# Products over 512 columns of weights in the gate stages and output projections of a two-layer decoder trunk

## The chip, the cores and the metric

The kernel runs on one core of one Trainium2 chip, in one launch. The metric is device time in microseconds (us). The five engines are TensorE (PE for matmuls, PEld for its weight loads), VectorE (DVE), ScalarE (ACT), GpSimd (POOL) and SyncE (SP, which issues the DMAs). They run beside each other and wait for each other by semaphores.

## The reference

x is 1024 tokens by 1024 channels, float32. The parts that the change touches are these, per layer:

```python
h = rmsnorm(x, norm_mix_pre[l])
if l % 2 == 0:                                     # layer 0
    proj = h @ w_in_even[e]
    qa, fa, ia, ga, ub, vb = jnp.split(proj, splits, axis=-1)   # 512 columns each
    oa = hgrn2_mix(qa, fa, ia, ga, ...)            # gated recurrence, ends with norm(o) * silu(ga)
    ob = chunk_gmlp_mix(gelu(ub), gelu(vb), ...)   # u * (W_s layernorm(v) + b), chunks of 128 tokens
    mix = jnp.concatenate([oa, ob], axis=-1) @ w_out_even[e]
else:                                              # layer 1
    mix = dilated_attention_mix(h, w_in_odd[o], positions) @ w_out_odd[o]
x = x + rmsnorm(mix, norm_mix_post[l])
h = rmsnorm(x, norm_ffn_pre[l])
y = jnp.square(jax.nn.relu(h @ w_ff1[l])) @ w_ff2[l]            # hidden size 4096
x = x + rmsnorm(y, norm_ffn_post[l])
```

## The kernel before

Every product is made of three matmuls in a short float32 format (fp32r): a weight or activation is split into a high part and the rest, and `mm3` (L624) adds hi·hi, hi·lo and lo·hi in one PSUM bank of 512 words. A weight piece is loaded by SP into a raw tile, ACT copies the high part, DVE or POOL subtracts it to get the rest (`load_piece`, L565). HT holds the layer's normalised input, transposed (channels as rows), in both parts.

`gemm_nat` (L631) is the product with tokens as rows: a 128x128 piece of HT is stationary, columns of weights move, and 8 channel blocks x 3 parts make 24 matmuls for one block of 128 tokens (t = 0 to 7). `gemm_tr` (L641) is the other way about: weights are stationary and 512 tokens move.

Layer 0's mixer (L844) has these stages in order: the value projection (256 columns a time), the recurrence in four heads (hgrn) with b products between its steps, then the stages b (gate input v, columns B0, normalised and mixed over the chunk: `gmlp_mix`), u (`gemm_tr`) and g (columns G0: the output gate of the recurrence, after which the two halves of the mixer's result are transposed into HT: `to_HT`, `ob_to_HT`). b and g are `gemm_nat` stages over 512 columns, which are taken as two runs of 256 (list `blocks`, L877): first all eight t for the first half, then all eight for the second. The output projection (L1374 to L1403) makes for each t and each half hf of the 1024 columns two `gemm_nat` products over 256 columns into the two halves of one bank; `post_part` squares and copies each bank, and after both halves the block's sum of squares, residual, second norm and h follow (`prenorm`), h is stored to DRAM (hd) and transposed into HT (`h_to_HT`). In layer 1 oT, the transposed attention output, is reloaded into HT from DRAM while the output projection has begun. Then `ff1` starts: hidden units are made in blocks i of 1024 (of 4096) from weights loaded as R tiles of 128x8x256 words (2048 words), each by two DMAs of 512 KB (`ff1_weights`, L1425); ACT copies and DVE subtracts a unit tile's two parts (128x1024 each) before its products start.

SBUF is handed out in numbered blocks: 17 of 1024 words, two of 2048 (b17 and b18) and some others (b7_14296 is tile 14296 in block 7). A tile gets a block when all earlier users of the block are done. R tiles need 2048 words, so only b17 and b18 take them.

All operations go through a recorder (`Plan`): the program first writes down every operation, and a list scheduler then gives them out at build time engine by engine, by readiness under a cost model, so that the order on each engine is fixed when the kernel runs. All instructions are issued at L422 (`emit`), which is the line that the profile shows. The names in it are the tiles: WP the ring of split weights, b the numbered blocks, mm, tr, pa, pb the banks.

Of the kernel before, what the change touches and what calls it, by code (L numbers as in the profile page):

```python
# [8 lines left out]
F32 = mybir.dt.float32  # L9
F32R = mybir.dt.float32r  # L10
# [474 lines left out]
class Trunk:  # L485
# [145 lines left out]
    def gemm_nat(self, t, w, c0, width, o=None):  # L631

        if o is None:
            o = self.mm_bank()[:, :width]
        ts = slice(t * P, (t + 1) * P)
        for k in range(NK):
            self.mm3(o, self.HT[:, 0, k, ts], self.HT[:, 1, k, ts],
                     w[0][k][0][:, c0:c0 + width], w[0][k][1][:, c0:c0 + width], k == 0, k == NK - 1)
        return o
# [204 lines left out]
    def layer0_mix(self):  # L844
# [3 lines left out]
        with nc.pool() as pl:  # L848
# [24 lines left out]
            for t, b in order:  # L873
                o = self.gemm_nat(t, wv[b], 0, 256)
                nc.scalar.activation(oa[t][:, b * 256:(b + 1) * 256], o, AF.Copy, scale=0.5)
            self.wfree(*wv)
            blocks = [("b", B0), ("b", B0 + 256), ("u", U0), ("u", U0 + 256), ("g", G0), ("g", G0 + 256)]  # L877
            ph = nc.pool()
            for h in range(4):
                state = None  # L880
                nxt = None
                for b in range(2):
                    fps = self.gemm_tr(b, wf, P)
                    qps = self.gemm_tr(b, wf, 0)
                    if b == 1:
                        self.wfree(wf)
                        nxt = (self.load_cols(w, [Q0 + (h + 1) * P, F0 + (h + 1) * P], P) if h < 3
                               else self.load_cols(w, [blocks[0][1]], 256))
# [6 lines left out]
            pl2.reserve("gz256", 256, F32, 2)  # L895
            vs = [pl2.tile([P, 512], F32, name="vs", bufs=NT) for t in range(NT)]
            ob = [[pl.tile([P, 2, 512], F32, name=f"ob{i}{j}") for j in range(2)] for i in range(2)]
            sums = {}
            for n, (kind, c0) in enumerate(blocks):
                nxt = None  # L900
                if n + 1 < len(blocks):
                    nxt = self.load_cols(w, [blocks[n + 1][1]], 256)
                else:
                    self.wout = [self.load_cols(a["w_out_even"][0], [256 * i], 256) for i in range(2)]
                half = n % 2
                cs = slice(half * 256, half * 256 + 256)
                if n == 2:
                    pl2.__exit__()
                    pl2 = nc.pool(2)
                if kind == "u":  # L910
                    for hf in range(2):
                        for j in range(2):
# [3 lines left out]
                            o = ob[hf][half][:, j]  # L916
                            nc.gpsimd.tensor_tensor(o, o, u, op=OP.mult)
                else:
                    for t in range(NT):
                        x = self.gemm_nat(t, cur, 0, 256)  # L920
                        if kind == "b":
                            if half == 0:
                                sums[t] = self.small(2)
                            self.gelu2(pl2, vs[t][:, cs], x, accum=sums[t][:, half:half + 1])
                            if half == 1:
                                self.gmlp_mix(t, ob, self.gmlp_norm(pl2, vs[t], sums[t]))
                        else:
                            if half == 0:
                                self.onorm(pl2, oa[t])
                            th = pl2.tile([P, 256], F32, name="th", tag="th", bufs=2)  # L930
# [892 lines left out]
```

## Time and profile before

| | |
|---|---|
| time, median of 3 runs | 2390.89 us (2390.3 to 2392.29) |
| time of the profiled execution | 2387.89 us |
| its span | 2385.8 us (2.09 us lie around it) |
| mean granted clock of PE | 0.988 of 2.4 GHz |
| busy: PE, PEld | 2291.6 us (96%), 2003.9 us (84%) |
| busy: DVE, ACT, POOL | 1627.4 us (68%), 1120.8 us (47%), 1095.5 us (46%) |

The busy share of PE is the mean over stages. The stages lie in the span as follows: layer 0's recurrence to 232 us, its stages b, u and g to 371, its output projection to 477, its feed-forward to 1098; layer 1's attention to 1595, output projection to 1728, feed-forward to the end. In a row of the timeline the first number is the start, the second the time until the last of the group ends, and the bracket at the end is the time that the engine idled before, with who released it.

### The profile page before, as it was taken

The numbers are of one execution on the slowest core, as the hardware profiler recorded it, in microseconds if no ns is written. First come the engines' busy times: TensorE is split into PE (matmuls) and PEld (weight loads), VectorE is DVE, ScalarE is ACT, GpSimd is POOL, SyncE is SP. The second block draws the span as 40 slices with busy tenths as digits, with TensorE's granted clock in tenths as the row PEclk, the third lists the DMA queues.
The fourth block names the chain that finished last, engine by engine and source line by source line (L and its number), as shares of the span: only waits on it lengthen the run. The fifth ranks groups of instructions, "written<-read, shape, count | busy, mean of one in ns | idle before, by whom it ended". The sixth has DMA issues, their size and how long they took to land.

```text
span 2385.8 us, 35511 instructions
## 1 busy us (share of the span) xinstructions
PE 2291.6 (96%) x12490; PEld 2003.9 (84%) x12490; DVE 1627.4 (68%) x3130; ACT 1120.8 (47%) x2429; POOL 1095.5 (46%) x1192
## 2 busy tenths in 40 slices
PE   8999999998999999999999999998998999999998
PEld 7888889976888878887999999988976888888887
DVE  6687875545555686748888788876645555778747
ACT  6444435442232343335777777787432223434333
POOL 2111343255655889415555455443245655555204
PEclk9999999999999999999999999999999999999999
DMA  5110123344444776854311111115444444678654
GB/s 186 54 36 19 36 71 121 142 167 156 158 146 150 242 249 240 287 192 155 102 48 51 46 47 52 46 57 176 167 147 158 160 150 150 251 274 285 220 175 166
DMA packets 229178, 342.33 MB, mean 143 GB/s; under 512 B 15220, under 2 KB 110472, under 8 KB 229000
## 3 DMA queue, kind: packets, MB, share of 16 engines
q1 hardware_dynamic: 229000, 340.07, 42.3%
q8 instruction: 98, 1.61, 0.3%
q14 instruction: 80, 0.66, 0.1%
HBM read 240.92 MB, written 99.09 MB: 143 GB/s over the span
## 4 chain that ended last, share of the span: by engine, by line
PE 74%; DVE 11%; POOL 4%; ACT 4%; DMA 4%; issue 2%; SPq 0%; DVEq 0%; POOLq 0%; ACTq 0%
PE mm L422 37%; PE pa L422 18%; PE pb L422 11%; DVE b L422 9%; PE tr L422 9%; POOL b L422 4%; ACT b L422 3%; DMA b<-hd 1%; DVE WP L422 1%; DMA b<-oTd 1%; DVE HT L422 1%; DMA b<-in_w_in_odd_dram 1%; ACT WP L422 1%; ACT HT L422 0%; DMA b<-in_w_ff_dram 0%
## 5 line engine op out<-in xcount | busy, mean ns | idle before, releaser
L422 POOL TENSOR_TENSOR b<-b,b 128x512 f32<-128x512 f32 (+5 forms) x522 | 590.3, 1146 | 750.4 <-ACT b L422 367.2
L422 PE MATMUL mm<-WP,HT 128*128 128x256 f32 (+2 forms) x4704 | 830.8, 323 | 7.4 <-DVE HT L422 3.2
L422 PEld LDWEIGHTS mm<-WP,HT 128*128 128x128 f32 x4704 | 710.4, 190 | 51.3 <-DVE HT L422 4.4
L422 ACT ACTIVATE b<-b 128x512 f32<-128x512 f32 (+6 forms) x659 | 326.0, 509 | 392.2 <-DVE b L422 158.8
L422 POOL TENSOR_TENSOR b<-b 128x512 f32<-128x512 f32 (+4 forms) x354 | 314.6, 894 | 334.7 <-DVE b L422 222.0
L422 ACT ACTIVATE WP<-b 128x1024 fp32r<-128x1024 f32 (+2 forms) x248 | 194.7, 792 | 350.8 <-PE pb L422 167.1
L422 DVE TENSOR_TENSOR WP<-b,WP 128x1024 fp32r<-128x1024 f32 (+1 forms) x164 | 234.6, 1436 | 150.6 <-ACT WP L422 150.3
L422 DVE TENSOR_TENSOR b<-b,b 128x1024 fp32r<-128x1024 f32 (+6 forms) x360 | 246.9, 703 | 123.1 <-ACT b L422 75.8
L422 ACT ACTIVATE b<-mm 128x512 f32<-128x512 f32 (+3 forms) x374 | 161.9, 445 | 263.4 <-PE mm L422 227.3
L422 PE MATMUL mm<-HT,b 128*128 128x512 f32 x1056 | 262.2, 399 | 17.3 <-ACT b L422 17.3
L422 PEld LDWEIGHTS mm<-HT,b 128*128 128x128 f32 x1056 | 200.4, 192 | 59.9 <-ACT b L422 19.3
L422 DVE TENSOR_TENSOR HT<-b,HT 128x1024 fp32r<-128x1024 f32 (+3 forms) x131 | 206.3, 1586 | 21.8 <-ACT HT L422 21.8
L422 PE MATMUL tr<-b,b 128*128 128x128 f32 x1074 | 176.6, 285 | 40.9 <-DVE b L422 33.8
L422 PE MATMUL pa<-WP,HT 128*128 128x512 f32 x768 | 193.7, 390 | 0.0
L422 DVE TENSOR_TENSOR b<-tr,b 64x128 fp32r<-64x128 f32 (+5 forms) x404 | 162.6, 407 | 36.2 <-ACT b L422 29.2
L422 PEld LDWEIGHTS tr<-b,b 128*128 128x128 f32 x1074 | 132.0, 150 | 61.5 <-DVE b L422 38.5
L422 PE MATMUL tr<-WP,HT 128*128 128x512 f32 x672 | 172.3, 394 | 6.7 <-ACT WP L422 3.6
L422 PEld LDWEIGHTS pa<-WP,HT 128*128 128x128 f32 x768 | 144.4, 188 | 30.0
L422 ACT ACTIVATE HT<-b 128x1024 fp32r<-128x1024 f32 (+4 forms) x147 | 142.1, 973 | 55.7 <-PE mm L422 23.5
L422 PE MATMUL pa<-WP,b 128*128 128x512 f32 x672 | 162.0, 389 | 0.0
L422 PEld LDWEIGHTS tr<-WP,HT 128*128 128x128 f32 x672 | 127.2, 190 | 34.6 <-ACT WP L422 4.0
L422 PE MATMUL pa<-b,b 128*128 128x128 f32 (+3 forms) x624 | 146.4, 333 | 5.5 <-DVE b L422 4.8
(62 smaller groups left out, 2872.8 us busy)
## 6 DMA issues: line engine op xcount, KB each, us to landing
b<-in_w_ff_dram SPq DMA_DIRECT2D x176, 512.0 KB, 4.8
hc<-b SPq DMA_DIRECT2D x224, 256.0 KB, 2.1
b<-hc SPq DMA_DIRECT2D x112, 512.0 KB, 5.5
b<-hd SPq DMA_DIRECT2D x56, 256.0 KB, 3.2
b<-in_w_in_odd_dram SPq DMA_DIRECT2D x64, 192.0 KB, 2.8
x<-b SPq DMA_DIRECT2D x24, 512.0 KB, 2.6
b<-x SPq DMA_DIRECT2D x24, 512.0 KB, 4.1
b<-in_w_in_even_dram SPq DMA_DIRECT2D x32, 256.0 KB, 2.8
```

Of the source, the lines that this page charges most:

```text
L422: return getattr(self.real[eng], meth)(*[x.real() if isinstance(x, View) else x for x in a], **{k: x.real() if isinstance(x, View) else x ...
```

## The change

Stages b and g are one run of 512 columns each instead of two of 256 (the list `blocks` carries a width), and each output projection product goes over 512 columns: 2304 matmuls of 128x256 become 1152 of 128x512 (384 each in the two gate stages together, in layer 0's output projection, and in layer 1's). What follows a product in b and g is done once on 512 columns instead of twice on 256 (gelu and its sum; tanh, add, multiply), and the add of the two half sums goes. w_out is loaded in four quarters (512 columns by half of the channels) in place of four runs of 256 columns. The quarter "wide", which lies outside the WP ring, is two tiles of 2048 words in place of four of 1024: b17 and b18. In layer 0 it is the quarter that the first half's products end with, (0, 1); in layer 1 it is (1, 1), which the second half's products end with.

```diff
--- before.py
+++ after.py
...
-    def gemm_nat(self, t, w, c0, width, o=None):
-
-        if o is None:
-            o = self.mm_bank()[:, :width]
+    def gemm_nat(self, t, w, width):
+
+        o = self.mm_bank()[:, :width]
         ts = slice(t * P, (t + 1) * P)
         for k in range(NK):
-            self.mm3(o, self.HT[:, 0, k, ts], self.HT[:, 1, k, ts],
-                     w[0][k][0][:, c0:c0 + width], w[0][k][1][:, c0:c0 + width], k == 0, k == NK - 1)
+            self.mm3(o, self.HT[:, 0, k, ts], self.HT[:, 1, k, ts], *w[k], k == 0, k == NK - 1)
         return o
...
-            blocks = [("b", B0), ("b", B0 + 256), ("u", U0), ("u", U0 + 256), ("g", G0), ("g", G0 + 256)]
+            blocks = [("b", B0, 512), ("u", U0, 256), ("u", U0 + 256, 256), ("g", G0, 512)]
...
-            sums = {}
-            for n, (kind, c0) in enumerate(blocks):
+            for n, (kind, c0, width) in enumerate(blocks):
                 nxt = None
                 if n + 1 < len(blocks):
-                    nxt = self.load_cols(w, [blocks[n + 1][1]], 256)
+                    nxt = self.load_cols(w, [blocks[n + 1][1]], blocks[n + 1][2])
                 else:
-                    self.wout = [self.load_cols(a["w_out_even"][0], [256 * i], 256) for i in range(2)]
-                half = n % 2
-                cs = slice(half * 256, half * 256 + 256)
-                if n == 2:
+                    self.wout = {(0, 0): self.load_cols(a["w_out_even"][0], [0], 512, (0, 2))}
...
-                        x = self.gemm_nat(t, cur, 0, 256)
+                        x = self.gemm_nat(t, cur[0], 512)
                         if kind == "b":
-                            if half == 0:
-                                sums[t] = self.small(2)
-                            self.gelu2(pl2, vs[t][:, cs], x, accum=sums[t][:, half:half + 1])
-                            if half == 1:
-                                self.gmlp_mix(t, ob, self.gmlp_norm(pl2, vs[t], sums[t]))
+                            s = self.small()
+                            self.gelu2(pl2, vs[t], x, accum=s)
+                            self.gmlp_mix(t, ob, self.gmlp_norm(pl2, vs[t], s))
                         else:
-                            if half == 0:
-                                self.onorm(pl2, oa[t])
-                            th = pl2.tile([P, 256], F32, name="th", tag="th", bufs=2)
+                            self.onorm(pl2, oa[t])
+                            th = pl2.tile([P, 512], F32, name="th", tag="th", bufs=2)
                             nc.scalar.activation(th, x, AF.Tanh, scale=0.5)
                             nc.vector.scalar_tensor_tensor(th, th, 1.0, x, op0=OP.add, op1=OP.mult)
-                            nc.gpsimd.tensor_tensor(oa[t][:, cs], oa[t][:, cs], th, op=OP.mult)
-                            if half == 1:
-                                self.to_HT(t, [oa[t][:, k * P:(k + 1) * P] for k in range(4)], t % 2 == 1)
-                                self.ob_to_HT(t, ob)
+                            nc.gpsimd.tensor_tensor(oa[t], oa[t], th, op=OP.mult)
+                            self.to_HT(t, [oa[t][:, k * P:(k + 1) * P] for k in range(4)], t % 2 == 1)
+                            self.ob_to_HT(t, ob)
...
-                    wnext = self.load_cols_lazy(self.a["w_out_odd"][0], [0], 256)
+                    wnext = self.load_cols_lazy(self.a["w_out_odd"][0], [0], 512, (0, 2))
...
-        self.wout = [wcur, self.load_cols_lazy(self.a["w_out_odd"][0], [256], 256)]
-        for x in self.wout:
+        self.wout = {(0, 0): wcur, (0, 1): self.load_cols_lazy(self.a["w_out_odd"][0], [0], 512, (4, 6))}
+        for x in self.wout.values():
...
-            self.wout.append(self.load_cols(wo, [512], 256))
-            self.wout.append(self.load_cols(wo, [768], 256, buf=[
-                pl.tile([P, 1024], F32R, name="wide", tag=f"wide{j}", bufs=1) for j in range(4)]))
+            wide = [pl.tile([P, 2048], F32R, name="wide", tag=f"wide{j}", bufs=1) for j in range(2)]
+            for x in ((0, 0), (0, 1), (1, 0), (1, 1)):
+                if x not in self.wout:
+                    buf = wide if x == ((1, 1) if l else (0, 1)) else None
+                    self.wout[x] = self.load_cols(wo, [512 * x[0]], 512, (4 * x[1], 4 * x[1] + 2), buf)
             n = 3 * l
             ss = {}
             for t, hf in sorted(((t, hf) for t in range(NT) for hf in range(2)), key=lambda x: (max(0, x[0] + 1 - n), x[1], x[0])):
-                bank = self.mm_bank()
-                for i in range(2):
-                    self.gemm_nat(t, self.wout[2 * hf + i], 0, 256, bank[:, 256 * i:256 * i + 256])
+                bank = self.gemm_nat(t, self.wout[hf, 0][0] + self.wout[hf, 1][0], 512)
...
-            self.wfree(*self.wout[:3])
+            self.wfree(*self.wout.values())
```

The scheduler gives out a new order. On SP, the loads of R tiles stand elsewhere. Before, in layer 1, two of them (here the second) were issued among the reloads of oT, a hundred microseconds ahead of ff1:

```order
L422 DMA oTd_71<-b18_6777 128x512 [waits DVE_49]
L422 DMA b19_14458<-oTd_71 128x4x128 [waits DMAHW0_49,DVE_49]
L422 DMA b7_14296<-oTd_71 128x4x128 [waits DMAHW6_49,DMAHW1_49,DVE_49]
L422 DMA b18_14731<-in_w_ff1_dram 128x4x256 [waits DMAHW7_49,DMAHW4_49]
L422 DMA b18_14731<-in_w_ff1_dram 128x4x256
L422 DMA b19_14458<-oTd_71 128x4x128 [waits DMAHW5_49,DVE_49]
L422 DMA b7_14296<-oTd_71 128x4x128 [waits DMAHW6_49,DMAHW2_49,DVE_49]
```

After, the first two stand behind the store of h of the seventh block (b12_13731 to hd_82; b17 and b18 are the blocks that wide held) and wait for PE, the last reader of wide:

```order
L422 DMA x3_70<-b0_13848 128x1024 [waits DMAHW3_49,DVE_49]
L422 DMA hd_82<-b12_13731 128x1024 [waits DMAHW0_49,DVE_49]
L422 DMA b17_14499<-in_w_ff1_dram 128x4x256 [waits PE_49,Pool_49]
L422 DMA b17_14499<-in_w_ff1_dram 128x4x256 [waits DMAHW2_49]
L422 DMA b18_14508<-in_w_ff1_dram 128x4x256 [waits PE_49,Pool_49]
L422 DMA b18_14508<-in_w_ff1_dram 128x4x256
L422 DMA x3_70<-b1_13859 128x1024 [waits DMAHW6_49,DMAHW5_49,DVE_49]
```

Both R pairs have moved behind wide's last matmul, which in layer 1 is the last one of the output projection. In layer 0 two R pairs, which SP issued at 49.24 us and among the loads of the g stage, likewise moved behind the last matmul on wide there, in the first half (hf = 0) of the eighth block.

On PE, at the end of the recurrence of layer 0 (pb, tr are its own matmuls, mm the b products), before:

```order
L422 MATMUL pb_81<-b9_542,b13_231 128x128 [waits DVE_49]
L422 MATMUL pb_81<-b2_94,b4_432 128x128
L422 MATMUL tr_78<-b2_94,b7_570 128x128 [waits Activation_49]
L422 MATMUL tr_77<-b2_94,b7_570 128x128
L422 MATMUL pb_81<-b19_689,b13_231 128x128 [waits DVE_49]
L422 MATMUL pb_81<-b2_94,b4_432 128x128
L422 MATMUL pb_81<-b19_689,b13_231 128x128 [waits DVE_49]
L422 MATMUL pb_81<-b3_95,b4_432 128x128
L422 MATMUL tr_78<-b3_95,b7_570 128x128
L422 MATMUL pb_81<-b9_542,b13_231 128x128 [waits DVE_49]
L422 MATMUL pb_81<-b3_95,b4_432 128x128
L422 MATMUL mm_76<-WP_67,HT_63 128x256 [waits DVE_49]
```

and after:

```order
L422 MATMUL tr_78<-b2_94,b7_570 128x128 [waits Activation_49]
L422 MATMUL tr_77<-b2_94,b7_570 128x128
L422 MATMUL mm_75<-WP_67,HT_63 128x512 x6
L422 MATMUL pb_81<-b19_687,b13_231 128x128 [waits DVE_49]
L422 MATMUL pb_81<-b2_94,b4_432 128x128
L422 MATMUL pb_81<-b19_687,b13_231 128x128 [waits DVE_49]
L422 MATMUL pb_81<-b3_95,b4_432 128x128
L422 MATMUL tr_78<-b3_95,b7_570 128x128
L422 MATMUL mm_75<-WP_67,HT_63 128x512 x3
L422 MATMUL mm_76<-WP_67,HT_63 128x512 x3
L422 MATMUL pb_81<-b9_542,b13_231 128x128 [waits DVE_49]
L422 MATMUL pb_81<-b3_95,b4_432 128x128
```

The three mm banks were full before, and the next b product waited for DVE to empty one; after, b products stand between the recurrence's steps to its end.

On PE, in layer 1's output projection, the transposes of the first block's h (tile b1_14522 before), before:

```order
L422 MATMUL mm_74<-WP_67,HT_63 128x256 [waits Activation_49]
L422 MATMUL mm_74<-WP_67,HT_63 128x256 x23
L422 MATMUL mm_74<-b5_14659,HT_63 128x256 x6
L422 MATMUL mm_74<-b2_14697,HT_63 128x256 x6
L422 MATMUL mm_74<-b0_14704,HT_63 128x256 x6
L422 MATMUL mm_74<-b3_14703,HT_63 128x256 x3
L422 MATMUL tr_77<-b20_87,b1_14522 128x128 [waits DVE_49]
L422 MATMUL tr_77<-b20_87,b1_14522 128x128 x3
L422 MATMUL mm_74<-b3_14703,HT_63 128x256 x3
L422 MATMUL tr_78<-b20_87,b1_14522 128x128 [waits DVE_49]
L422 MATMUL tr_78<-b20_87,b1_14522 128x128 x3
L422 MATMUL mm_75<-WP_67,HT_63 128x256 [waits Activation_49]
```

and after (b3_13716):


```order
L422 MATMUL mm_75<-WP_67,HT_63 128x512 x12
L422 MATMUL mm_75<-b17_13824,HT_63 128x512 x6
L422 MATMUL mm_75<-b18_13891,HT_63 128x512 x6
L422 MATMUL mm_74<-WP_67,HT_63 128x512 [waits Activation_49]
L422 MATMUL mm_74<-WP_67,HT_63 128x512
L422 MATMUL mm_74<-WP_67,HT_63 128x512 [waits DVE_49]
L422 MATMUL mm_74<-WP_67,HT_63 128x512 x9
L422 MATMUL tr_77<-b20_87,b3_13716 128x128 [waits DVE_49]
L422 MATMUL tr_77<-b20_87,b3_13716 128x128 x3
L422 MATMUL mm_74<-WP_67,HT_63 128x512 x3
```

Before, they stand behind 21 of the 24 matmuls of 256 columns on wide in the third block's second half; after, behind all of that half and 12 matmuls of 512 columns of the next product.

## Rows read from the trace of the kernel before

**Rows 1.** The page: the span, and the chain that ended last, by engine

```profile
span 2385.8 us, 35511 instructions
...
PE 74%; DVE 11%; POOL 4%; ACT 4%; DMA 4%; issue 2%; SPq 0%; DVEq 0%; POOLq 0%; ACTq 0%
```

**Rows 2.** Windows: length, busy us of PE, PEld, DVE, ACT, POOL, granted clock

```profile
225.00:264.00 39.00, 35.32 (x285) 34.23 (x286) 23.09 (x92) 15.06 (x39) 5.15 (x4) 1.00 0.09 28
264.00:326.00 62.00, 59.33 (x318) 50.41 (x319) 61.34 (x236) 30.05 (x106) 31.75 (x24) 1.00 0.18 52
...
371.00:477.40 106.40, 104.64 (x875) 103.86 (x874) 60.01 (x117) 53.77 (x128) 27.63 (x23) 1.00 0.39 137
1595.00:1726.00 131.00, 119.90 (x929) 114.93 (x930) 86.00 (x183) 83.10 (x177) 41.90 (x41) 0.96 0.51 165
```

**Rows 3.** Lines by form, PE: count, then busy us and mean ns

```profile
L422 PE MATMUL mm<-WP,HT 128*128 128x256 f32 x2304 | 298.3, 286 | 7.1 <-DVE HT L422 3.2 <-DVE b L422 2.9 <-ACT b L422 0.6
...
L422 PE MATMUL mm<-WP,HT 128*128 128x512 f32 x864 | 218.8, 389 | 0.0
...
L422 PE MATMUL mm<-b,HT 128*128 128x256 f32 x384 | 50.8, 286 | 0.0
```

**Rows 4.** Timeline, PE, two back-to-back runs: start, us, count, idle before

```profile
232.11 27.61 PE L422 MATMUL mm<-WP,HT 128*128 128x256 f32 x228 [1.64 <-DVE b L422]
259.56 1.06 PE L422 MATMUL tr<-b,b 128*128 128x128 f32 x8
...
296.25 29.53 PE L422 MATMUL mm<-HT,WP 128*128 128x512 f32 x129
325.62 4.59 PE L422 MATMUL mm<-WP,HT 128*128 128x256 f32 x37
```

**Rows 5.** Timeline, PE, end of layer 0's recurrence: the first of six waits

```profile
223.38 0.68 PE L422 MATMUL pa<-b,b 128*128 128x128 f32 x4 [0.23 <-DVE b L422]
```

**Rows 6.** Timeline, PE, first stages after it: first and last of five POOL waits

```profile
263.85 0.38 PE L422 MATMUL tr<-b,b 128*128 128x128 f32 x1 [1.08 <-POOL b L422]
...
292.24 1.16 PE L422 MATMUL tr<-b,b 128*128 128x128 f32 x8 [0.52 <-POOL b L422]
```

**Rows 7.** Timeline, PE, ACT: layer 1's wait for the first h, and its window

```profile
1652.50 2.68 PE L422 MATMUL mm<-b,HT 128*128 128x256 f32 x21
1661.45 1.12 PE L422 MATMUL tr<-b,b 128*128 128x128 f32 x4 [6.27 <-DVE b L422]
...
1656.12 2.04 ACT L422 ACTIVATE HT<-b 128x512 fp32r<-128x512 f32 x2
...
1657.00:1664.00 7.00, 2.55 (x12) 2.55 (x13) 6.22 (x13) 4.96 (x11) 1.26 (x1) 0.55 0.56 173
```

**Rows 8.** Timeline, PE, the two starts of the first feed-forward products

```profile
477.37 5.75 PE L422 MATMUL mm<-HT,b 128*128 128x512 f32 x24 [1.72 <-ACT b L422]
485.67 3.23 PE L422 MATMUL mm<-HT,b 128*128 128x512 f32 x9 [2.55 <-ACT b L422]
488.70 1.83 PE L422 MATMUL tr<-b,b 128*128 128x128 f32 x8
...
560.75 2.93 PE L422 MATMUL mm<-HT,b 128*128 128x512 f32 x6 [4.32 <-ACT b L422]
...
1729.56 5.74 PE L422 MATMUL mm<-HT,b 128*128 128x512 f32 x24 [1.78 <-ACT b L422]
1738.04 0.97 PE L422 MATMUL mm<-HT,b 128*128 128x512 f32 x3 [2.74 <-ACT b L422]
```

**Rows 9.** Timeline, SP: an early load; DMA issues at 436:440, median to landing

```profile
1625.79 0.93 SPq L422 DMA_DIRECT2D b<-in_w_ff_dram  x2
...
b<-in_w_ff_dram SPq DMA_DIRECT2D x2, 512.0 KB, 6.4
```

**Rows 10.** Timeline, ACT and DVE: the two splits of one such piece

```profile
475.21 1.04 ACT L422 ACTIVATE b<-b 128x1024 fp32r<-128x1024 f32 x1
...
1726.03 1.23 DVE L422 TENSOR_TENSOR b<-b,b 128x1024 fp32r<-128x1024 f32 x1 [0.65 <-PE mm L422]
```

More of the change, by code (lines that the diff above doesn't have):

```diff
@@ L873, in layer0_mix @@
             for t, b in order:
-                o = self.gemm_nat(t, wv[b], 0, 256)
+                o = self.gemm_nat(t, wv[b][0], 256)
                 nc.scalar.activation(oa[t][:, b * 256:(b + 1) * 256], o, AF.Copy, scale=0.5)
             self.wfree(*wv)
-            blocks = [("b", B0), ("b", B0 + 256), ("u", U0), ("u", U0 + 256), ("g", G0), ("g", G0 + 256)]
+            blocks = [("b", B0, 512), ("u", U0, 256), ("u", U0 + 256, 256), ("g", G0, 512)]
             ph = nc.pool()
@@ L887, in layer0_mix @@
                         nxt = (self.load_cols(w, [Q0 + (h + 1) * P, F0 + (h + 1) * P], P) if h < 3
-                               else self.load_cols(w, [blocks[0][1]], 256))
+                               else self.load_cols(w, [blocks[0][1]], blocks[0][2]))
                     state = self.hgrn(ph, h, b, fps, qps, oa, state)
@@ L894, in layer0_mix @@
             pl2 = nc.pool(2)
-            pl2.reserve("gz256", 256, F32, 2)
             vs = [pl2.tile([P, 512], F32, name="vs", bufs=NT) for t in range(NT)]
             ob = [[pl.tile([P, 2, 512], F32, name=f"ob{i}{j}") for j in range(2)] for i in range(2)]
-            sums = {}
-            for n, (kind, c0) in enumerate(blocks):
+            for n, (kind, c0, width) in enumerate(blocks):
                 nxt = None
                 if n + 1 < len(blocks):
-                    nxt = self.load_cols(w, [blocks[n + 1][1]], 256)
+                    nxt = self.load_cols(w, [blocks[n + 1][1]], blocks[n + 1][2])
                 else:
-                    self.wout = [self.load_cols(a["w_out_even"][0], [256 * i], 256) for i in range(2)]
-                half = n % 2
-                cs = slice(half * 256, half * 256 + 256)
-                if n == 2:
+                    self.wout = {(0, 0): self.load_cols(a["w_out_even"][0], [0], 512, (0, 2))}
+                if n == 1:
                     pl2.__exit__()
@@ L915, in layer0_mix @@
                             self.gelu2(pl2, u, x)
-                            o = ob[hf][half][:, j]
+                            o = ob[hf][n - 1][:, j]
                             nc.gpsimd.tensor_tensor(o, o, u, op=OP.mult)
@@ L963, in gmlp_norm @@
         mu = self.small(nm="mu")
-        nc.vector.tensor_tensor(mu, sums[:, 0:1], sums[:, 1:2], op=OP.add)
-        nc.vector.tensor_scalar(mu, mu, -1.0 / 512, None, op0=OP.mult)
+        nc.vector.tensor_scalar(mu, sums, -1.0 / 512, None, op0=OP.mult)
         vn = pool.tile([P, 512], F32, name="vn", tag="vn", bufs=3)
```

## Prediction

> **What bounds the kernel now.** I read the page's chain first: 74% of it is PE [rows 1], so a saved PE microsecond is a saved microsecond unless something else ends last in that stage. The windows say where that holds [rows 2]. Layer 0's output projection is PE alone: 104.64 of 106.4 us busy. Layer 1's has 11.1 us of PE idle (131.0 − 119.90), so a wait matters there too. In the b and u stages (225 to 326 us) PE is idle for 6.35 of 101 us, but DVE is busy for 61.34 of 62 us in the second of the two windows: a second candidate for the bound. Then the PE timeline at each seam: the end of the recurrence [rows 5], the first stages behind it [rows 6], the first h of layer 1 [rows 7] and the two starts of the feed-forward products [rows 8].
>
> **The matmuls.** 228 of 256 columns take from 232.11 to 259.56 us, 120.4 ns each; 129 of 512 take from 296.25 to 325.62 us, 227.7 ns each [rows 4]. Two of the first cost 240.8 ns, so each merged pair gives 13.1 ns. Of 256 columns there are 2304 + 384 matmuls [rows 3]; less the 384 of the value projection, which stay, 2304 are paired. 1152 x 13.1 ns = 15.1 us, and 5.0 each in the gates, in layer 0's and in layer 1's output projection. Busy time bounds it: per matmul 129.5 ns (298.3/2304), 132.3 (50.8/384) and 253.2 (218.8/864) [rows 3], which gives 6.7 us from the first and third and 13.0 from the second and third; but these ends are modelled, so I take the starts. Above, the gain can hardly pass 20 us, if the fixed part of a 256 (120.4 − 106.7 = 13.7 ns, 106.7 being 256 columns at the full 2.4 GHz) went from one of each pair and the longer matmul hid some of its own.
>
> The fixed part is what the change buys, and the Trainium skill speaks against its size: "TensorE: Matmul & The Clock Gate", section "Wait — 56ns, not 53.3ns?", has a matmul at full clock cost its columns at 2.4 GHz plus about 2.5 ns. By that a pair saves 2.5 ns and the change 2.9 us. The rows differ: 13.7 ns at 256 columns and 14.4 at 512.
>
> **The vector work.** Gelu, tanh, the adds and multiplies of b and g go over the same elements in half as many instructions. It lies beside PE, which hides it; I cost it at nothing. If that cover is gone (DVE as the bound of the u stage) the third case below holds.
>
> **The end of the recurrence.** PE waits six times from 223.38 to 232.11 us, the last time 1.64 us, 3.8 us in all [rows 4, 5], because all three mm banks hold b products and the recurrence itself runs on DVE. A product now is 24 x 227.7 ns = 5.5 us of filler for a bank, not 2.9. The new order has b products between the recurrence's steps until its end: −3 us (0 to −3.8; a step of the recurrence can come up to three matmuls, 0.7 us, late behind a filler, which takes some of it).
>
> **Waits for POOL.** Five waits for the mixing matrices' operand sum to 3.75 us from 263.85 to 292.24 [rows 6]. Each block's norm and mix now begin after one product and not in the second run over all t, so they fall into a stretch where DVE is busy for 23.09 of 39 us and POOL for 5.15 [rows 2]. I take −1.5 (−3.75 if all go; +3 if DVE, full in the u stage, makes PE wait for the first block of g).
>
> **Layer 1's first h.** PE waits 6.27 us before 1661.45 for the first block's h. Ahead of that chain on ACT stand copies of reloaded oT, as at 1656.12 for 2.04 us; these pieces come from DRAM, so its end doesn't move with the matmuls. The transposes now stand behind 3 matmuls of 256 and 12 of 512 more: 0.36 + 2.73 = 3.1 us that fill the wait. But 144 pairs lie ahead of it, and their 1.9 us end in it. Net −1.2; and the clock, which is 0.55 in the mean over the window around the wait [rows 7], is back sooner: −2 (0 to −4).
>
> **Pieces of w_out.** As many bytes in as many DMAs. Layer 1's wide needs b18, which a store of the attention's output holds until about then; PE can go on with the next product. +0.3 (0 to +3).
>
> **The feed-forward starts.** Here the change gives time back. Wide takes b17 and b18, the only homes of an R tile. Before, two R pairs lay in SBUF long ahead (in layer 1 from 1625.79) [rows 9], and PE's first ff1 product came 1.72 and 1.78 us after the output projection's last matmul (475.65 and 1727.78) [rows 8]. Now SP issues them when wide is read for the last time. A pair lands 6.4 us after issue [rows 9], and then come ACT's 1.04 and DVE's 1.23 us [rows 10]: 8.7 us. Behind the waiting load on SP stand the store of the eighth block's h and the next R pair. In layer 0 wide is done one product (5.5 us) ahead of the end, so its first unit comes about 3.2 us after the end in place of 1.7. In layer 1 nothing is in front: about 7 to 9 us in place of 1.8.
>
> What this costs is less than the idle time. These products only fill the time until the eighth block's transposes (488.70, which is 13.05 us after the end [rows 8]); and at 560.75 PE waits 4.32 us for the activations that follow from that h [rows 8]. So work that slips behind the transposes partly falls into idle time, and what counts is how much later the transposes are. New splits now stand before the eighth block's norm on ACT and DVE; two of each (2 x 1.04, 2 x 1.23) make it 1 to 3 us late. Layer 0: +2 (0 to +6). Layer 1: +3.5 (+1 to +7), with a stretch at half clock after the longer idle.
>
> **Sum.** −15.1 − 3 − 1.5 − 2 + 0.3 + 2 + 3.5 = −15.8 us. The profiled execution took 2387.89 us (2.09 around its span [rows 1]), so 2372.1 by its own time; it is 3.0 us under the median, 2390.89, and from the median it is 2375.
>
> **Rivals.**
> - *The gain comes whole* and the filler hides the starts: −15.1 − 3.8 − 3.75 − 4 + 2 = −24.7: 2366. For it: the transposes come 13 us after the end, longer than the 8.7 a load needs. Against: the extra splits in that chain.
> - *The gates aren't bound by PE.* Their 5.0 us and the 4.5 at the seams go into DVE's time; −15.8 + 9.5 = −6.3: 2385. For: 61.34 of 62 us. Against: DVE has 16 us idle in the window before, where the mixes now go.
> - *Slower: the late R tiles.* Each start stands for a whole load: 8.7 − 1.7 = 7.0 us, about 3 us more at half clock (as the 0.55 over 7 us [rows 7]), and all of it reaches the eighth block's transposes: 10 us a layer, 20 in both. Without the gains at the seams −15.1 + 20 + 0.3 = +5: 2396. It decides from 15 us for both starts, 7.5 a layer. For: in layer 1 there is nothing else for PE to do. Against: in layer 0 one product lies in front, and part of the slipped work falls into the later wait.
> - *The skill's 2.5 ns.* A pair saves little because the fixed part is not per matmul: −2.9 − 6.5 + 5.8 = −3.6: 2387. Both rows 4 at 13.7 and 14.4 ns speak against it.
>
> That the change doesn't do what it says is excluded by the order: 1152 matmuls of 512 stand where 2304 of 256 did.
>
> **Chances.** Forecast (2368 to 2382) 0.56; whole gain 0.14; gates not bound 0.14; late R tiles 0.12; small fixed part 0.04. A measurement of this kernel tells 0.2%, 4.8 us, from no change: faster means under 2386.1. Faster: 0.56 + 0.14 + 0.10 of the gates' case = 0.80. Same (to 2395.7): 0.04 of that case, 0.03 of the small fixed part, 0.05 of the late R tiles = 0.12. Slower: the rest, 0.08. The range leaves out the lower end of the whole gain and most of the late R tiles: 2365 to 2390; the forecast's own is 2368 to 2382.
>
> **What would show it.** 24 matmuls of 512 from start to start in 5.46 us in both output projections; no waits of PE at the recurrence's end; the wait before layer 1's first transposes at about 5 us; the first ff1 product some 3 us after layer 0's end and 7 to 9 after layer 1's; the eighth block's transposes 14 to 15 us after it. It is wrong if PE waits more than 4 us in the gates, if a 512 steps by more than 235 ns, or if the two starts cost over 10 us.

## The result, and the profile after

The changed kernel takes 2375.39 us (median of 4 runs) against 2390.6 us of the kernel before (median of 4 runs): ratio 0.9937, 95% interval 0.9923 to 0.9951, 15.2 us less. One of the four runs of the changed kernel took 4596.13 us, in a slow state, and the ratio leaves it out. The other three took 2369.33 to 2375.49. Timed a second time beside the kernel before, the changed kernel had the ratio 0.9933 (0.9920 to 0.9947). The forecast was 2375 (2365 to 2390). The total is right; several of its terms are not, and they nearly cancel.

The profiled execution of the changed kernel took 2375.28 us. Its page (span; engines), and the line by form that now holds the merged matmuls (864 + 960 of them; 192 more are `mm<-b`):

```profile
span 2373.5 us, 33100 instructions
...
PE 2281.4 (96%) x11338; PEld 1941.4 (82%) x11338; DVE 1610.0 (68%) x3090; ACT 1116.5 (47%) x2405; POOL 1088.0 (46%) x1184
```

```profile
L422 PE MATMUL mm<-WP,HT 128*128 128x512 f32 x1824 | 459.9, 395 | 0.4 <-DVE HT L422 0.4
```

PE is busy for 10.2 us less than in the table of before and DVE for 17.4; the share of PE is 96% as before. Between the profiled executions the span is 12.3 us shorter; the medians are 15.2 apart, mostly because the execution profiled before lay 2.7 under the median of its four runs, 2390.6.

The same marks in both traces (us from the span's start; the gain at a mark is all that was won up to there):

| mark | before | after | gain |
|---|---|---|---|
| layer 0, first matmul of the output projection | 376.17 | 366.71 | 9.5 |
| layer 0, end of its last matmul | 475.65 | 464.86 | 10.8 |
| layer 0, ff1 product after the long wait | 560.75 | 549.65 | 11.1 |
| layer 0, feed-forward's second part, a product where its stalls end | 914.46 | 904.87 | 9.6 |
| layer 0, last products of the feed-forward | 1094.13 | 1086.44 | 7.7 |
| layer 1, first matmul of the output projection | 1596.41 | 1590.05 | 6.4 |
| layer 1, transposes of the first h | 1661.45 | 1650.55 | 10.9 |
| layer 1, end of the output projection | 1727.78 | 1714.68 | 13.1 |
| layer 1, ff1 product after the long wait | 1817.34 | 1804.24 | 13.1 |
| end of the span | 2385.8 | 2373.5 | 12.3 |

What a stretch gave is the difference between the gains at its two ends. A second execution of the changed kernel, profiled later, comes 0.6 to 2.3 us earlier at these marks and 3.6 us at the end of the span, so differences of about 1 us between two traces say little.

**The gates** gave what was forecast (9.5; 10.1 in the second execution). Timeline, PE, end of the recurrence and the mixes' waits, which answers to [rows 4 to 6]:

```profile
233.50 0.61 PE L422 MATMUL pb<-b,b 128*128 128x128 f32 x4
233.87 7.77 PE L422 MATMUL mm<-WP,HT 128*128 128x512 f32 x33
...
245.23 1.16 PE L422 MATMUL tr<-b,b 128*128 128x128 f32 x8 [0.56 <-POOL b L422]
...
288.67 1.16 PE L422 MATMUL tr<-b,b 128*128 128x128 f32 x8 [0.41 <-POOL b L422]
...
327.70 0.66 PE L422 MATMUL tr<-b,b 128*128 128x128 f32 x4 [3.16 <-POOL b L422]
```

None of the six waits at the recurrence's end is left. Of the waits for POOL four remain in the b and u stages (0.20 to 0.69, 1.9 us in all, before 3.8), but stage g has a new one of 3.16 us; the one of 1.29 that it had before is gone. In all PE waits 5.0 us in these stages, as before. PE waits there for POOL's multiply of the first block's gate, and POOL waits for DVE:

```profile
326.38 1.26 POOL L422 TENSOR_TENSOR b<-b,b 128x512 f32<-128x512 f32 x1 [0.69 <-DVE b L422]
```

Splits of weights and operations of the norms stand ahead of that block on DVE, and splits of w_out's pieces on ACT. Behind the wait the granted clock of PE is half for 3.4 us (a window row with the columns of [rows 2]; the clock is 0.50):

```profile
328.70:332.10 3.40, 3.40 (x10) 2.62 (x9) 2.06 (x4) 1.20 (x3) 2.93 (x3) 0.50 0.60 166
```

In the second execution the wait is 3.02 us and the clock stays at 1.00 behind it; from the end of the wait to the output projection it takes 37.4 us there and 39.0 here, 1.6 us more.

**The matmuls.** In layer 1, 12 of 512 columns from start to start:

```profile
1638.62 2.88 PE L422 MATMUL mm<-WP,HT 128*128 128x512 f32 x12
1641.34 2.88 PE L422 MATMUL mm<-b,HT 128*128 128x512 f32 x12
...
1644.06 2.88 PE L422 MATMUL mm<-WP,HT 128*128 128x512 f32 x12
1650.55 1.11 PE L422 MATMUL tr<-b,b 128*128 128x128 f32 x4 [3.62 <-DVE b L422]
```

2.72 us for 12, 226.7 ns each, as forecast (227.7). The wait for the first h is 3.62 us, where it was 6.27 [rows 7]; about 5 was forecast. The whole output projection of layer 1 takes 6.9 us less from its first to its last matmul (124.2 for 131.1).

**The output projections** gave 1.3 us in layer 0 between the first two marks, not 5.0. The matmuls did save 5.5 there (93.5 us from start to start before, 88.0 after), but PE has new waits between the two halves of a block's transposes. PE, DVE and POOL of the changed kernel at one of them:

```profile
397.57 0.60 PE L422 MATMUL tr<-b,b 128*128 128x128 f32 x4
398.92 0.66 PE L422 MATMUL tr<-b,b 128*128 128x128 f32 x4 [0.75 <-DVE b L422]
```

```profile
396.38 2.48 DVE L422 SCALAR_TENSOR_TENSOR b<-b,b,b 128x512 f32<-128x512 f32 x2
```

```profile
397.04 1.28 POOL L422 TENSOR_TENSOR b<-b,b 128x512 f32<-128x512 f32 x1 [4.15 <-ACT b L422]
```

```profile
397.05 1.81 DVE L422 SCALAR_TENSOR_TENSOR b<-b,b,b 128x512 f32<-128x512 f32 x1
```

DVE writes h in two scalar_tensor_tensor of 512 columns; the last row is the second one alone. The pair takes 2.48 us: POOL's multiply of `post_part` begins 0.01 us ahead of the second one and runs to 398.32, and the second one ends 0.54 us after that. In the kernel before the two met as well, but there the second one began first (at 470.06). The pair took 1.42 us, and POOL's multiply, which came 0.98 us after the pair's start, took longer:

```profile
469.39 1.42 DVE L422 SCALAR_TENSOR_TENSOR b<-b,b,b 128x512 f32<-128x512 f32 x2
```

```profile
470.37 1.59 POOL L422 TENSOR_TENSOR b<-b,b 128x512 f32<-128x512 f32 x1 [4.47 <-ACT b L422]
```

There are four such waits in layer 0 (0.75 us each, 3.0 in all; from start to start the transposes take 4.1 us more) and three in layer 1 (2.3). POOL's being first does not by itself make PE wait. In layer 1 of the kernel before there are three such pairs, here the first, and PE had matmuls ahead of the transposes and did not idle:

```profile
1685.01 1.29 POOL L422 TENSOR_TENSOR b<-b,b 128x512 f32<-128x512 f32 x1 [4.79 <-ACT b L422]
1685.17 2.34 DVE L422 SCALAR_TENSOR_TENSOR b<-b,b,b 128x512 f32<-128x512 f32 x2
1686.90 1.32 PE L422 MATMUL tr<-b,b 128*128 128x128 f32 x8
```

**The feed-forward starts**, which answer to [rows 8]:

```profile
466.22 5.73 PE L422 MATMUL mm<-HT,b 128*128 128x512 f32 x24 [1.36 <-ACT b L422]
474.10 5.30 PE L422 MATMUL mm<-HT,b 128*128 128x512 f32 x15 [2.15 <-ACT b L422]
479.24 0.60 PE L422 MATMUL tr<-b,b 128*128 128x128 f32 x4
```

```profile
549.65 2.93 PE L422 MATMUL mm<-HT,b 128*128 128x512 f32 x6 [4.32 <-ACT b L422]
```

```profile
1719.90 8.23 PE L422 MATMUL mm<-HT,b 128*128 128x512 f32 x24 [5.22 <-ACT b L422]
1727.98 1.03 PE L422 MATMUL tr<-b,b 128*128 128x128 f32 x8
```

```profile
1804.24 2.93 PE L422 MATMUL mm<-HT,b 128*128 128x512 f32 x6 [4.65 <-ACT b L422]
```

The first product comes 1.4 us after the end in layer 0 (forecast 3) and 5.2 in layer 1 (7 to 9); the eighth block's transposes 14.4 and 13.3 us after it (14 to 15; before 13.05 and 11.8). From the end of the output projection to the product after the long wait it is 84.8 us in layer 0 (before 85.1) and 89.6 in layer 1 (before 89.6). By these marks the starts cost nothing, where 5.5 us were forecast. In layer 1 PE idles 5.22 us in one piece ahead of the eighth block's transposes, where before it idled 1.78, 2.74 and 0.59 us.

**A stall far from the change.** In layer 0's feed-forward, between 780 and 1000 us, waits of PE (us in total, times, longest), before and after:

```profile
PE tr L422 <- ACT WP L422: 3.6, 1, 3.6
PE tr L422 <- DVE WP L422: 2.8, 1, 2.8
```

```profile
PE tr L422 <- DVE b L422: 10.0, 1, 10.0
PE pa L422 <- DVE b L422: 0.5, 1, 0.5
```

The two waits of before became one of 10.0 us. With smaller pieces PE idles 10.5 us in this window, 6.5 before. PE, the window behind the wait with its granted clock, and DVE at its end, in the changed kernel:

```profile
904.87 2.93 PE L422 MATMUL tr<-WP,HT 128*128 128x512 f32 x6 [9.99 <-DVE b L422]
```

```profile
904.80:909.00 4.20, 4.13 (x10) 3.30 (x11) 2.63 (x4) 0.00 (x0) 4.12 (x3) 0.50 0.71 253
```

```profile
901.25 0.29 DVE L422 TENSOR_SCALAR b<-b 128x256 int32<-128x256 int32 x1 [12.61 <-POOL b L422]
901.46 1.42 DVE L422 TENSOR_TENSOR HT<-b,HT 128x1024 fp32r<-128x1024 f32 x1
902.80 1.41 DVE L422 TENSOR_TENSOR WP<-b,WP 128x1024 fp32r<-128x1024 f32 x1
904.14 1.28 DVE L422 TENSOR_TENSOR b<-tr,b 128x512 f32<-128x512 f32 x2
```

Layer 1's mask tiles are built there, partly on POOL (iota) and partly on DVE (a bitwise and). DVE stands 12.61 us at that small operation; behind it in its queue are split weights and the emptying of the bank (b<-tr) for which PE waits. On POOL the iota of that tile stands behind two subtractions for split weights. The new order moved this chain on POOL and DVE. On PE the order of the feed-forward is that of before up to 816.80 us (806.32 after); from there on the first products of its second part stand in another order too, mm and tr in turn by six matmuls where there were 18 of mm in a row. From the product after the long wait to the last products of the feed-forward the changed kernel takes 536.8 us, 3.4 more than before; in the second execution it is 2.7 more.

### The profile page after: what moved, and what is told of

Its sections match the earlier page's. It is cut to its first block, busy times and chain, and to the rows that moved or that the text cites. A ratio compares the mean times of both kernels' runs of the same rounds, so it can differ in the third digit from the quotient of the medians.

```text
span 2373.5 us, 33100 instructions
## 1 busy us (share of the span) xinstructions
PE 2281.4 (96%) x11338; PEld 1941.4 (82%) x11338; DVE 1610.0 (68%) x3090; ACT 1116.5 (47%) x2405; POOL 1088.0 (46%) x1184
## 5 line engine op out<-in xcount | busy, mean ns | idle before, releaser
L422 POOL TENSOR_TENSOR b<-b,b 128x512 f32<-128x512 f32 (+4 forms) x505 | 572.6, 1150 | 699.5 <-ACT b L422 346.5
L422 PE MATMUL mm<-WP,HT 128*128 128x512 f32 (+2 forms) x3744 | 826.8, 363 | 2.0 <-DVE HT L422 1.2
L422 PEld LDWEIGHTS mm<-WP,HT 128*128 128x128 f32 x3744 | 655.6, 190 | 79.9 <-DVE HT L422 2.3
L422 ACT ACTIVATE b<-b 128x128 f32<-128x128 f32 (+6 forms) x651 | 325.0, 513 | 376.1 <-POOL b L422 167.8
L422 POOL TENSOR_TENSOR b<-b 128x512 f32<-128x512 f32 (+4 forms) x363 | 321.6, 893 | 381.8 <-DVE b L422 239.8
L422 DVE TENSOR_TENSOR HT<-b,HT 128x1024 fp32r<-128x1024 f32 (+3 forms) x131 | 190.8, 1467 | 19.5 <-ACT HT L422 19.5
```

Of the source, the lines that this page charges most:

```text
L422: return getattr(self.real[eng], meth)(*[x.real() if isinstance(x, View) else x for x in a], **{k: x.real() if isinstance(x, View) else x ...
```

## The experiments

All were timed in five rounds beside the kernel before; ratios are to it, on the same chip. The first four ran on one chip and the last four on another.

**Gates alone** (output projections as before). Of the diff against the kernel before:

```diff
-            blocks = [("b", B0), ("b", B0 + 256), ("u", U0), ("u", U0 + 256), ("g", G0), ("g", G0 + 256)]
+            blocks = [("b", B0, 512), ("u", U0, 256), ("u", U0 + 256, 256), ("g", G0, 512)]
...
-                    self.wout = [self.load_cols(a["w_out_even"][0], [256 * i], 256) for i in range(2)]
+                    self.wout = [self.load_cols(a["w_out_even"][0], [0], 256)]
```

> Only the gate stages b and g go over 512 columns; the output projections stay as before (two products over 256 columns in one bank; their loads of columns 256 to 511 start after stage g instead of in it). Theory from the two traces: the start of layer 0's output projection is 9.5 us earlier, of which 5.0 are the matmuls and 4.5 the waits at the end of the recurrence and for POOL; nothing later changes, so about 2381 us (9.5 under before). Rival: the seams give nothing and only the matmuls count: 5 us, 2385.6. Second rival: the late pieces of w_out cost up to 3 us of it.

Measured: 0.9975 (0.9965 to 0.9985), 6 us. That lies between the theory's 9.5 and the rival's 5. In its trace the output projection starts at 364.27, 11.9 us earlier than before, more than the theory and 2.4 earlier than in the changed kernel: its waits in stage g are 1.83 and 0.33 us in place of 3.16, and the clock stays at 1.00 there. The output projection takes 0.5 us longer than before, so the second rival's late pieces cost no more than that. Later PE waits 10.2 us at 903 us as in the changed kernel, and the sum of its waits from 780 to 1000 is 11.3 us (6.5 before). The theory of the seams holds at its place; that nothing later changes was wrong: of 11.9 us, 8.6 are left at the end of the span.

**Output projections alone** (gates as before). Of the diff against the changed kernel:

```diff
-            blocks = [("b", B0, 512), ("u", U0, 256), ("u", U0 + 256, 256), ("g", G0, 512)]
+            blocks = [("b", B0), ("b", B0 + 256), ("u", U0), ("u", U0 + 256), ("g", G0), ("g", G0 + 256)]
```

> Only the output projections go over 512 columns (with their weight quarters and the two tiles of 2048 words for wide); stages b and g stay as before. Theory from the two traces: the matmuls give 5 us a layer, but new waits of PE for the second half of h (0.75 us each, four in layer 0, three in layer 1) take most of it back, and the late R tiles cost about nothing: 3 to 5 us in all, 2386 to 2388. Rival, the terms as predicted (10 of matmuls, 2 at the first h, less 5.8 at the feed-forward starts): 6.5 us, 2384. Rival, late R tiles as dear as feared: no gain or slower.

Measured: 0.9997 (0.9988 to 1.0005): no change. The theory's 3 to 5 us were too many, and so were the first rival's 6.5. Its trace has six waits of 0.75 us in layer 0's output projection and three in layer 1's (6.8 us), and one of 11.5 us at 918 us. So the matmuls' 10 us are about eaten by these and the stall. No change is what the last rival said, but its cause does not show: from the end of the output projection to the product after the long wait it is 85.2 and 88.8 us, before 85.1 and 89.6.

**post_part's multiply on DVE**, in the changed kernel's output projections. The number that `post_part` gets decides the engine; the larger one also drops ACT's copy of the bank.

```diff
-                self.post_part(pl, t, hf, bank, ys[t], gpost, ss[t])
+                self.post_part(pl, NT + t, hf, bank, ys[t], gpost, ss[t])
```

> The changed kernel, with the multiply of post_part in the two output projections on DVE, straight from the bank, instead of ACT's copy and POOL's multiply. Theory: in the changed kernel POOL's multiply runs beside DVE's second scalar_tensor_tensor of h and stretches it from 0.7 to 1.8 us, and PE waits 0.75 us for the second four transposes, seven times in all; without POOL's multiply these go: the seven waits under 0.2 us each, and 4 to 7 us faster than the changed kernel, about 2369 to 2371. Rival: the second half of h is late because the transposes now stand back to back without matmuls between them, whatever POOL does: the waits stay at 0.5 us or more and the time at 2375.

Measured: 0.9909 (0.9895 to 0.9922), 6 to 7 us under the changed kernel's 0.9933 and 0.9937. DVE and PE at the place shown above:

```profile
394.73 1.42 DVE L422 SCALAR_TENSOR_TENSOR b<-b,b,b 128x512 f32<-128x512 f32 x2
```

```profile
396.03 1.04 PE L422 MATMUL tr<-b,b 128*128 128x128 f32 x8
```

The pair is back at 1.42 us and all eight transposes run without a wait, although they stand back to back; in neither output projection does PE idle between transposes (0.0 us). Layer 0's takes 94.1 us in place of 98.2, 4.1 less, and layer 1's 119.9 in place of 124.6. The theory holds, the rival falls: it was POOL's multiply. Back-to-back transposes alone bring no wait; and the rows at 1685 us of the kernel before show none where POOL was first but PE had matmuls ahead of the transposes.

**Wide in four tiles of 1024 words**, so that b17 and b18 stay with the R tiles.

```diff
-            wide = [pl.tile([P, 2048], F32R, name="wide", tag=f"wide{j}", bufs=1) for j in range(2)]
+            wide = [pl.tile([P, 1024], F32R, name="wide", tag=f"wide{j}", bufs=1) for j in range(4)]
...
-                    b, buf = buf[0], buf[1:]
+                    bs, buf = buf[:2], buf[2:]
...
+                    pairs = [(x[:, :n], x[:, n:2 * n]) for x in bs]
```

> The changed kernel, with wide in four tiles of 1024 words (one channel block each) instead of two of 2048, so that the R tiles keep blocks b17 and b18 and are loaded far ahead as in the kernel before. Theory from the two traces: the late R tiles cost nothing net, since the wait in front of the second block's products (560.75 before, 549.65 after) kept its distance from the end of the output projection within 0.3 us: same time within 2 us, 2373 to 2377, though the first ff1 product comes 1.8 us after the output projection instead of 5.2 in layer 1. Rival (the predicted 2 and 3.5 us): 5 us faster, 2370.

Measured: 0.9886 (0.9873 to 0.9898), 11 to 12 us under the changed kernel. The theory falls, and the rival's 5 us are too few. PE at the two starts, and its waits from 780 to 1000 us:

```profile
462.77 5.75 PE L422 MATMUL mm<-HT,b 128*128 128x512 f32 x24 [1.32 <-ACT b L422]
469.54 0.66 PE L422 MATMUL tr<-b,b 128*128 128x128 f32 x4 [1.02 <-DVE b L422]
```

```profile
1702.13 5.74 PE L422 MATMUL mm<-HT,b 128*128 128x512 f32 x24 [1.27 <-ACT b L422]
1710.27 3.28 PE L422 MATMUL mm<-HT,b 128*128 128x512 f32 x9 [2.40 <-ACT b L422]
```

```profile
PE tr L422 <- DVE WP L422: 2.5, 2, 1.7
PE mm L422 <- DVE b L422: 2.2, 1, 2.2
PE tr L422 <- DVE b L422: 1.5, 1, 1.5
PE tr L422 <- ACT WP L422: 0.5, 1, 0.5
```

The span is 2357.8 us, 15.7 under the changed kernel's first execution and 12.1 under its second, which is nearer to the ratios. Against the second the difference builds up so: 2.8 us by the end of layer 0's output projection (the wait in stage g is 1.45 us in place of 3.02); 1.8 to the product after the long wait; 3.9 in the rest of layer 0's feed-forward, where PE's waits from 780 to 1000 are 6.7 us in place of 10.5; 2.1 in the attention; 2.2 in layer 1's output projection; and from there to the end 0.6 the other way.

At the starts themselves the early R tiles are worth little. In layer 0 it is 82.7 us from the end of the output projection to the product after the long wait, against 84.8 and 84.5 in the two executions with late tiles: 2 us. The order there is another one too (the eighth block's transposes come 8.1 us after the end and not 14.4), so that it is the loads alone is not shown. In layer 1 it is 88.6 against 89.6 and 88.3: no cost can be seen. Most of the 11 to 12 us lies in shorter waits away from the starts; what makes each was not tried.

**The changed kernel again**, as the reference on the chip of the last four.

> The changed kernel once more, on the chip on which the next three run, so that they have it as a reference: 0.9937 of the kernel before, within its interval 0.9923 to 0.9951 (14 to 16 us less).

Measured: 0.9933 (0.9920 to 0.9947), 2371.76 us. Its trace, the second execution above, has the same waits (9.6 us at 903; four and three of 0.75).

**Pairs of 256 in the changed kernel.**

```diff
-        for k in range(NK):
-            self.mm3(o, self.HT[:, 0, k, ts], self.HT[:, 1, k, ts], *w[k], k == 0, k == NK - 1)
+        for c in range(0, width, 256):
+            cs = slice(c, c + 256)
+            for k in range(NK):
+                self.mm3(o[:, cs], self.HT[:, 0, k, ts], self.HT[:, 1, k, ts],
+                         w[k][0][:, cs], w[k][1][:, cs], k == 0, k == NK - 1)
```

> The changed kernel with each product over 512 columns made again of two runs of 256 in the same bank; loads, tiles, banks and the vector work stay merged. It prices the matmuls alone. Theory (13.1 ns a pair, 1152 pairs, PE the bound in these stages): 15 us slower than the changed kernel, nearly the time before; a little less where the longer fillers hide the 0.75 us waits for the second half of h (seven of them, up to 5 us). Rival (the gain is the seams and the 512 columns themselves give 2.9 us): 3 us slower than the changed kernel. Rival (the stages are bound by DVE and POOL): the same time as the changed kernel.

Measured: 0.9991 (0.9983 to 1.0000), 2385.95 us, 14.2 slower than the changed kernel beside it. These are nearly the 15 us of the theory, and the two rivals fall; but the places are not where it put them. In layer 0's output projection the matmuls take 5.1 us longer (93.2 for 88.0 from start to start), which is the price that was forecast, and layer 1's takes 5.0 longer as a whole (129.7 for 124.6). To the end of layer 0's output projection, however, the difference is 3.5 us (467.78 against 464.27) and not 10, since this kernel has no waits between transposes in either output projection (at most 0.19 us). The rest comes at layer 1's first h, where the difference grows from 5.6 to 9.8 us, and behind it, to 13.6 at the end. So that the sum comes out near 15 is in part luck. The gates of this kernel, without the 512, start the output projection at 368.65: 7.5 us of the 9.5 (or 10.1) come without them, with the merged vector work, the fuller banks and the new order, and 2 to 2.6 us with the longer matmuls, where 5.0 were forecast. Its wait in stage g is 1.74 us; the longer one of the changed kernel takes part of the rest.

**Mask work off DVE**, in the changed kernel.

```diff
-            self.nc.vector.tensor_scalar(e, d, 3, None, op0=OP.bitwise_and)
+            G.tensor_copy(e, d)
...
-            self.nc.vector.tensor_scalar(e, d, 15, None, op0=OP.bitwise_and)
+            G.tensor_copy(e, d)
```

> The changed kernel with DVE's two small integer operations of each mask tile (built for layer 1 in layer 0's feed-forward) replaced by copies on POOL; this leaves the stride test out of the mask, so the output is another. Theory: DVE waits for POOL's iota there (up to 12.6 us at a time) and holds up the split weights behind it, for which PE waits 9.99 us at 905 us in the changed kernel; without DVE's part that wait goes: 6 to 10 us faster than the changed kernel. Rival: the wait comes from the weights' DMA or from POOL's own queue, and stays: the time is the changed kernel's within 3 us.

Measured: 0.9914 (0.9901 to 0.9928), 2368.81 us, 3 us under the changed kernel beside it: less than the theory's 6 to 10, and at the edge of the rival's "within 3".

```profile
PE mm L422 <- DVE b L422: 4.9, 1, 4.9
PE tr L422 <- DVE b L422: 1.8, 1, 1.8
PE pa L422 <- DVE b L422: 0.5, 1, 0.5
```

The wait of 10 us is gone, so DVE's stand at POOL's iota made it. Another of 4.9 us came at 991 us: 7.2 us in all. Whether that one belongs to the stage or to this edit, which gives POOL two more copies for each mask tile, is open. From the product after the long wait to the last products of the feed-forward this kernel takes 0.6 us longer than the kernel before, where the changed kernel takes 3.4 and 2.7 longer: by this measure the stand cost 2 to 3 us.

**Both edits** (four wide tiles, multiply on DVE).

> Both edits that made the changed kernel faster: wide in four tiles of 1024 words (R tiles early) and the post_part multiply of the output projections on DVE. Theory: they act on different waits (the feed-forward starts and the second half of h), so the waits of 0.75 to 1.0 us that the first alone still has in the output projections (4.2 us in all) go as well: 4 us under the first alone, about 0.987 of the kernel before. Rival: they share their gain (both shift the mask's place in the feed-forward, which is where most of it came from): the first alone's 0.9886.

Measured: 0.9856 (0.9842 to 0.9871), 2356.55 us against 2388.35: 32 us under the kernel before and 15 under the changed one on the same chip, the fastest here. The waits between transposes in the output projections fall from 4.0 us to 0.8. Under the first edit alone, which ran on another chip, it is 0.0030 (7 us) by the ratios, 0.0020 (5 us) by the medians and 2.5 us by the spans of the two profiles; 4 were expected. So the second edit adds something to the first, against the rival, but how much is not settled, and neither is it shown that the two gains (11 to 12 and 6 to 7 us) add up in full.

## Why the prediction was right, and where it was not

- *Matmul step.* 13.1 ns a pair was right: 120.0 and 226.7 ns from start to start, and 5.5 us less matmul time in layer 0's output projection. The Trainium skill's 2.5 ns ("TensorE: Matmul & The Clock Gate", "Wait — 56ns, not 53.3ns?") gives an estimate of 2.9 us for the whole change; the rows have 13 ns a pair, and the kernel with pairs of 256 was 14.2 us slower.
- *Gates.* Forecast 5.0 + 3 + 1.5 = 9.5, measured 9.5. Its parts differ. All six waits at the recurrence's end are gone (3.8 for 3), but the waits behind them are 5.0 us as before: 1.9 fewer for POOL in b and u, 3.16 new in g. More than 4 us of waits in the gates was one of the forecast's signs of being wrong, and it showed. What the forecast had named as a risk, +3 if DVE makes PE wait for the first block of g, came true. 7.5 us come without the longer matmuls and about 2 to 2.6 with them. That DVE is the bound of these stages as a whole did not come true.
- *Layer 1's first h and output projection.* The wait shrank by 2.65 us, forecast 1.2 (2 with the clock). The whole output projection gave 6.9 us, forecast 5.0 + 2 − 0.3 = 6.7. That it fits is luck in part: three new waits (2.3 us) stand against smaller waits early in it (2.4 us in place of 4.6).
- *Layer 0's output projection: the step that failed.* Forecast 5.0, measured 1.3. "Layer 0's output projection is PE alone" was true before and not after. I counted h's chain as moved with the matmuls, and did not ask whether POOL's multiply would still begin after DVE's second write of h, nor what PE has to do between a block's transposes. Four waits, 3.0 us (4.1 from start to start), were shown by putting the multiply on DVE.
- *The feed-forward starts.* Forecast +2 and +3.5. The eighth block's transposes are 1.3 and 1.5 us later, as forecast (1 to 3), but by the marks nothing of it reaches the product after the long wait. Against the kernel with early tiles the starts cost about 2 us in layer 0, with another order there, and nothing that can be told from the scatter in layer 1. The idle time in layer 1 was as described (5.2 us, the clock 0.81 in the window from 1712 to 1730), but PE had idled 5.1 us ahead of the same transposes before, in three pieces.
- *Not in the sum at all:* layer 0's feed-forward, where 3.4 us are lost. PE idles 4 us more there (6.5 to 10.5) behind the mask chain, with a stretch at half clock after it. The forecast did not look at the order there, on PE, DVE or POOL.
- *The total* is right in part by luck. By the marks the change gave 12.3 us and not 15.8: 3.7 less than forecast in layer 0's output projection, 3.4 in its feed-forward, 1.3 in the attention and 0.8 at the end, against 5.8 that were charged to the starts and did not come. The medians differ by 15.2 all the same, since the profiled execution of before, from which the marks are taken, was 2.7 us under its median.

## What to carry to other kernels

A saved fixed part per matmul is real where PE bounds the stage, but it moves the phase of everything beside it: look in the new order for pairs of two-input operations on DVE and POOL that meet, and for which of the two now begins first; here 0.01 us decided it. In a kernel whose order is planned at build time, compare all engines over the whole program, not only the stages edited: 3.4 us of the gain were lost 400 us later. Try a scratch tile in smaller blocks, too: with wide's four tiles of 1024 words the kernel was 11 to 12 us faster, though only about 2 of them lie at the starts for which it was tried.

## What was not expected of the hardware

A DVE operation with SBUF inputs that came up 0.01 us after a multiply on POOL was held for most of that multiply: the second scalar_tensor_tensor took 1.81 us in place of 0.75 and ended 0.54 us after POOL's multiply (398.86 after 398.32). The other way about POOL paid: its multiply took 1.59 us where it began during DVE's second operation, and 1.28 where it was first. That is what the Trainium skill says of the port pair of the two ("SBUF — State Buffer", "SBUF: two separate sides"): whoever begins first holds it for the whole instruction. The rows agree on who pays, in both directions; the late one ends a little sooner after the other than its own time alone (0.54 and 0.75 us; 1.15 and 1.28).

Two executions of one kernel also differed in the clock: half for 3.4 us behind a wait of 3.16 us in stage g, and full behind a wait of 3.02 us at the same place, which made 1.6 us.
